# Weight buffers at four different places modulo 512 bytes, in a two-layer decoder trunk

## The chip, the cores and the metric

The kernel runs on one core of one Trainium2 chip. The metric is the device time of one execution, in microseconds. Two runs of the kernel before took 1301.53 and 1301.77 us, median 1301.65 us. TensorE appears as PE (matmuls) and PEld (loads of the stationary operand), VectorE as DVE, ScalarE as ACT, GpSimd as POOL, SyncE as SP; SPq and ACTq are the DMA-issuing instructions of these engines.

## The reference, cut to what matters

Two layers over 256 positions of width 2048, all in float32. The even layer projects x with one wide matrix, feeds a state-space mixer (SSD) and a causal attention over one block of 256 positions, joins both and projects back. The odd layer is a diagonal complex state-space mixer (S5) with a gated unit (GLU) between two projections. Each ends in a LayerNorm.

```python
def reference(x, ...):
    for layer in range(DEPTH):                      # DEPTH = 2
        if layer % 2 == 0:
            h = ssd_moba_mixer(x, in0_w, ..., out0_w)   # x @ w_in ... concat([y_a, y_b]) @ w_out
        else:
            h = s5_mixer(x, in1_w, ..., glu_w, out1_w)  # x @ w_in, scan, gelu(y) @ w_glu, ... @ w_out
        x = layer_norm(DEEPNORM_ALPHA * x + h, ln_g[layer], ln_b[layer])
    return x
```

## The kernel before, in words

**Units of weights.** All projections read their weights in units of 128 partitions x 1024 float32 (4096 bytes per partition). `split_to` (L252) issues, for each unit, one DMA from SP into a buffer `raw` (L275), then `split` (L242) makes two parts of it in TensorE's fp32r format: ACT copies the unit to `wh` (the high part, L236) and DVE subtracts, `wl = raw - wh` (the low part, L244). The three tags `raw`, `wh` and `wl` lie in the pool `st` (L184) with four buffers each. A few units, whose numbers lie in `keep[1]`, get buffers of their own in another pool, because they are used twice or late.

**Products.** A product of float32 accuracy is the sum of three fp32r matmuls: high by high, high by low, low by high. In `xmm` (L323) the activations are the stationary operand (128 columns, 512 bytes per partition) and the weights stream through, 512 columns (2048 bytes) a matmul. In `pairmm` (L331, L334) the weights are stationary, and the activations stream through: 512 columns for the high part of the weights, 256 for the low part. The GLU's groups 1 to 3 have a form of their own (L1624, with weights streaming). The activations lie in the large slots `AB`, `CF` and `D`.

**What sets the order.** The program is written as a sequence of calls; a scheduler then fixes the order of instructions on each engine, from the calls' order, a simulated timeline and the moment at which a buffer of a pool comes free there. On the chip each engine runs its list strictly in that order and waits on semaphores. Before the change a new `wh` or `wl` takes whichever of the four buffers of its tag comes free first; so the order of the buffers is not a fixed rotation, and where two units are used out of turn the later one needn't wait for the earlier.

**Addresses.** In the program as built, the four `raw`, the four `wh` and the four `wl` all start at multiples of 512 bytes in a partition (`wh` at 119808, 123904, 128000 and 132096), and so do `AB`, `CF` and `D`. The slices that the fp32r matmuls read are 512 bytes, 1024 bytes or 2048 bytes long and start at such multiples too. A tile `pad` of 160 bytes in the first pool (L479) sets where the rest begins.

**Two places that the text below speaks of.** (1) The output projection of the even layer, 641 to 727 us into the span, where POOL, DVE and SP also prepare tables for the odd layer: `bc`, a tile of 256 KB, is loaded by SP at L806; DVE reads it at L820 and L821 into `tm`, and sums `tm` into `bb` at L823; `ft` and `bb` go through small matmuls at L857. (2) The change from one GLU group to the next, some 1158 us into the span: `end` (L1652 to L1657) adds the PSUM tiles of the group on DVE, and the next group's first matmul writes the PSUM bank that L1654 has read.

Of the kernel before, what the change touches and what calls it, by code (L numbers as in the profile page):

```python
# [9 lines left out]
F32 = mybir.dt.float32  # L10
F32R = mybir.dt.float32r
# [5 lines left out]
P = 128  # L17
# [3 lines left out]
UK = 2  # L21
# [4 lines left out]
STEPS = [0, 1, 4, 2, 5, 6, 3, 7]  # L26
WARM0 = 10
PAD = 40
FIRST = 3
EPS = 1e-5  # L30
NEG = -1e30
# [139 lines left out]
def trunk(tc, io, out):  # L171
# [4 lines left out]
    def nm(s):  # L176
        count[0] += 1
        return f"{s}_{count[0]}"

    with ExitStack() as top:  # L180
# [3 lines left out]
        st = enter(tc.tile_pool(name="st", bufs=4))  # L184
# [19 lines left out]
        def big(tag, shape, dt=F32):  # L204
            return slot.tile(shape, dt, tag=tag, name=nm(tag))

        units = []
        for name in ("wi0", "wo0", "wi1", "wglu", "wo1"):
            units += [io[name][i] for i in range(io[name].shape[0])]
# [5 lines left out]
        keep = [None, range(0)]  # L215
# [35 lines left out]
        def split_to(i):  # L251
            while nsplit[0] <= min(i, len(units) - 1):  # L252
                n = nsplit[0]
                if n in early:
                    early.pop(n)()
                if n in special:
                    special.pop(n)(n)
                    continue
                raw = st.tile([P, UK, 512], F32, tag="raw", name=nm("raw"))
                if n == 0:  # L260
                    wh = st.tile([P, UK, 512], F32R, tag="wh", name=nm("wh"))
                    wl = st.tile([P, UK, 512], F32R, tag="wl", name=nm("wl"))
                    for k in range(UK):
                        chained(nc.sync, nc.sync.dma_start, raw[:, k, :], units[n][:, k * 512 : k * 512 + 512])
                    for k in range(UK):
                        xpart(k)
                        chained(A, A.activation, wh[:, k, :], raw[:, k, :], AF.Copy)
                        chained(V, V.tensor_tensor, wl[:, k, :], raw[:, k, :], wh[:, k, :].bitcast(F32), op=OP.subtract)
                    ready[n] = (wh, wl)
                    nsplit[0] += 1  # L270
                    continue
                if n == FIRST + 1:
                    for e in (nc.sync, A, V):
                        line.pop(e, None)
                f = chained if nc.sync in line else lambda e, f, *a: f(*a)  # L275
                lastraw[0] = f(nc.sync, nc.sync.dma_start, raw.rearrange("p k n -> p (k n)"), units[n])
                at = room.get(n, n)
                pool, th, tl = (keep[0], f"wh{at % 8}", f"wl{at % 8}") if at in keep[1] else (st, "wh", "wl")
                wh = pool.tile([P, UK, 512], F32R, tag=th, name=nm("wh"))
                wl = pool.tile([P, UK, 512], F32R, tag=tl, name=nm("wl"))  # L280
                split(n, raw, wh, wl)

        jobs = deque()
# [200 lines left out]
        with ExitStack() as l0:  # L484
# [172 lines left out]
            ta = fmem[:, 2304:3072].rearrange("p (a n) -> p a n", a=3)  # L657
            tb = fmem[:, 3072:4096].rearrange("p (a n) -> p a n", a=4)
# [504 lines left out]
        with ExitStack() as lt:  # L1163
            tp = lt.enter_context(tc.tile_pool(name="tp", bufs=1))
# [128 lines left out]
        with ExitStack() as l1:  # L1293
# [287 lines left out]
            forms, fx, gp, set0 = more["f"], more["x"], more["p"], more["s"]  # L1581

            def fast_unit(raws, second):
                def go(n):
                    raw = st.tile([P, UK, 512], F32, tag="raw", name=nm("raw"))
                    lastraw[0] = nc.sync.dma_start(raw.rearrange("p k n -> p (k n)"), units[n])
                    if not second:
                        wh, wl = (st.tile([P, UK, 512], F32R, tag=t, name=nm(t)) for t in ("wh", "wl"))
                        raws[0] = raw
                        split(n, raw, wh, wl)  # L1590
                        return
                    wh, wl = (fx.tile([P, 1, 512], F32R, tag=t, bufs=2, name=nm(t)) for t in ("bh", "bl"))
                    ra = raws[0]
                    ta, tb = (fx.tile([P, 2, 512], F32, tag="mix", bufs=2, name=nm("mix")) for _ in range(2))
                    V.tensor_tensor(ta, ra, raw[:, 1:2, :].to_broadcast([P, 2, 512]), op=OP.subtract)
                    V.tensor_tensor(tb[:, 0, :], ta[:, 1, :], ra[:, 0, :], op=OP.add)
                    V.tensor_tensor(tb[:, 1, :], raw[:, 0, :], tb[:, 0, :], op=OP.subtract)
                    got = [(wh, wl)]
                    A.activation(wh[:, 0, :], raw[:, 0, :], AF.Copy)
                    V.tensor_tensor(wl[:, 0, :], raw[:, 0, :], wh[:, 0, :].bitcast(F32), op=OP.subtract)  # L1600
                    for t, pool, bufs in ((ta, fx, 2), (tb, st, 4)):
                        th, tl = (pool.tile([P, UK, 512], F32R, tag=tag, bufs=bufs, name=nm(tag)) for tag in ("wh", "wl"))
                        high = A.activation(th, t, AF.Copy)
                        low = V.tensor_tensor(tl, t, th.bitcast(F32), op=OP.subtract)
                        got.append((th, tl))
                    splits[n] = (high, low)
                    ready[n] = got
                    nsplit[0] += 1
                return go
# [122 lines left out]
        with ExitStack() as l2:  # L1732
# [56 lines left out]
            def last():  # L1789
                t = 1  # L1790
                mr = mr1[:, t]
                chain = []

                def then(f, *args, **kw):
                    with ExitStack() as pin:
                        if chain:
                            pin.enter_context(tc.issue_after(chain[-1].ins))
                        chain.append(f(*args, **kw))

                pf = [tpp.tile([P, 512], F32, name=f"tail{i}")[:, 0:NB] for i in range(2)]  # L1800
                for i in range(2):
                    T.matmul(pf[i], ident, xg[:, i, :], start=True, stop=False)
                low, high = x1[:, t, 1536 : 1536 + S], x1[:, t, 1536 + S :]
                then(V.scalar_tensor_tensor, x1[:, t, 1536:], x1[:, t, 1536:], ALPHA, ps_t[t][t], op0=OP.mult, op1=OP.add)
                then(V.bn_stats, st1[:, t, 3, :], low)
                then(V.tensor_tensor, high, high, ps_t[t][2][:, S:], op=OP.add)
                then(V.bn_stats, st1[:, t, 4, :], high)
                then(V.bn_aggr, mr[:, 0:2], st1[:, t, :, :].rearrange("p a b -> p (a b)"))
                then(V.tensor_scalar, mr[:, 2:3], mr[:, 1:2], EPS, None, op0=OP.add)
                dg = tp.tile([P, 2, P], F32, name="dg")  # L1810
                first = A.activation(dg[:, 0, :], ident, AF.Copy, scale=mr[:, 0:1])
                with tc.issue_after(first.ins):
                    root = A.activation(mr[:, 3:4], mr[:, 2:3], AF.Sqrt)
                with tc.issue_after(root.ins):
                    A.activation(dg[:, 1, :], ident, AF.Copy, scale=mr[:, 3:4])
                sls = [slice(2 * NB + sum(NV[:i]), 2 * NB + sum(NV[: i + 1])) for i in range(len(NV))]

                def centre(i):
                    xv = x1[:, t, sls[i]]
                    then(V.scalar_tensor_tensor, xv, xv, mr[:, 0:1], gb1[:, 0, sls[i]], op0=OP.subtract, op1=OP.mult)  # L1820

                def rescale(i):
                    xv = x1[:, t, sls[i]]
                    then(V.scalar_tensor_tensor, xv, xv, mr[:, 2:3], gb1[:, 1, sls[i]], op0=OP.mult, op1=OP.add)
                    nc.sync.dma_start(out[t * P : t * P + P, sls[i]], xv)

                centre(0)
                then(V.reciprocal, mr[:, 2:3], mr[:, 3:4])
                for i in range(2):
                    T.matmul(pf[i], dg[:, 0, :], gn[:, i, :], start=False, stop=False)  # L1830
                for i in range(2):
                    T.matmul(pf[i], dg[:, 1, :], gb1[:, 1, NB * i : NB * i + NB], start=False, stop=True)
                rescale(0)
                for i in range(1, len(NV)):
                    centre(i)
                    rescale(i)
                for i in range(2):
                    sl = slice(NB * i, NB * i + NB)
                    A.activation(x1[:, t, sl], pf[i], AF.Copy, scale=mr[:, 2:3])
                    nc.scalar.dma_start(out[t * P : t * P + P, sl], x1[:, t, sl])  # L1840
# [29 lines left out]
```

## Time and profile before

| what | value |
|---|---|
| median of the two runs | 1301.65 us |
| the profiled execution's own time | 1301.36 us |
| its span (first to last instruction) | 1299.5 us |
| around the span (the difference) | 1.9 us |
| matmuls, busy PE | 7998, 1292.1 us |
| busy DVE, ACT, POOL | 1038.5, 704.6, 424.5 us |
| granted TensorE clock, mean | 0.999 |
| splits on ACT (L236), mean of one | 425, 1058 ns |
| splits on DVE (L244), mean of one | 425, 1251 ns |

A matmul's duration in the profile (about 390 ns for 512 columns) contains its latency; what a matmul costs when it stands in a row of others is the distance from its start to the next one's start. The chain of work that ended last counts it so: in a row of it, the time divided by the count is the cost of one.

### The profile page before, as it was taken

The numbers are of one execution on the slowest core, as the hardware profiler recorded it, in microseconds if no ns is written. First come the engines' busy times: TensorE is split into PE (matmuls) and PEld (weight loads), VectorE is DVE, ScalarE is ACT, GpSimd is POOL, SyncE is SP. The second block draws the span as 40 slices with busy tenths as digits, with TensorE's granted clock in tenths as the row PEclk, the third lists the DMA queues.
The fourth block names the chain that finished last, engine by engine and source line by source line (L and its number), as shares of the span: only waits on it lengthen the run. The fifth ranks groups of instructions, "written<-read, shape, count | busy, mean of one in ns | idle before, by whom it ended". The sixth has DMA issues, their size and how long they took to land.

```text
span 1299.5 us, 21574 instructions
## 1 busy us (share of the span) xinstructions
PE 1292.1 (99%) x7998; PEld 1093.2 (84%) x7998; DVE 1038.5 (80%) x1575; ACT 704.6 (54%) x972; POOL 424.5 (33%) x665
## 2 busy tenths in 40 slices
PE   9999999999999999999999999999999999999998
PEld 8888888887888888888888888888888888888886
DVE  6889848798798788889878766749998857878876
ACT  6666669965654544544554345743355555554442
POOL 0060000124028659749788720034432200000100
PEclk9999999999999999999999999999999999999999
DMA  8655675555657857858867787497988665556872
GB/s 324 199 163 179 198 264 194 159 182 179 208 186 248 261 190 251 271 178 269 304 219 250 241 264 248 138 345 241 328 307 297 209 222 184 183 185 227 279 227 94
DMA packets 92106, 295.47 MB, mean 227 GB/s; under 512 B 11536, under 2 KB 18704, under 8 KB 91744
## 3 DMA queue, kind: packets, MB, share of 16 engines
q1 hardware_dynamic: 73696, 249.57, 58.1%
q0 software_dynamic: 8224, 32.81, 7.4%
q10 hardware_dynamic: 10080, 11.71, 2.9%
q8 instruction: 63, 1.03, 0.3%
q14 instruction: 43, 0.35, 0.1%
HBM read 272.78 MB, written 21.27 MB: 226 GB/s over the span
## 4 chain that ended last, share of the span: by engine, by line
PE 96%; POOL 2%; DVE 1%; ACT 1%; issue 0%; DMA 0%; ACTq 0%; POOLq 0%
PE main L323 37%; PE main L331 26%; PE main L334 13%; PE more L1624 7%; PE main L1624 3%; PE main L1263 2%; PE aux L331 1%; PE aux L956 1%; POOL CF L573 1%; PE aux L857 1%; POOL CF L572 1%; PE enc L1383 1%; PE dec L1428 1%; PE aux L334 1%; PE aux L459 1%; PE aux L1043 1%
## 5 line engine op out<-in xcount | busy, mean ns | idle before, releaser
L236 ACT ACTIVATE wh<-raw 128x1024 fp32r<-128x1024 f32 x425 | 447.8, 1058 | 447.7 <-PE main L323 176.4
L244 DVE TENSOR_TENSOR wl<-raw,wh 128x1024 fp32r<-128x1024 f32 x425 | 529.5, 1251 | 195.2 <-ACT wh L236 189.4
L331 PE MATMUL main<-AB,wh 128*128 128x512 f32 x1344 | 347.2, 394 | 0.0
L331 PEld LDWEIGHTS main<-AB,wh 128*128 128x128 f32 x1344 | 238.7, 189 | 41.6 <-issue 1.1
L323 PE MATMUL main<-wh,CF 128*128 128x512 f32 (+1 forms) x768 | 240.0, 391 | 0.0
L334 PEld LDWEIGHTS main<-AB,wl 128*128 128x128 f32 x1344 | 189.5, 190 | 17.4 <-issue 0.2
L323 PE MATMUL main<-wh,AB 128*128 128x512 f32 x640 | 202.0, 392 | 0.0
L334 PE MATMUL main<-AB,wl 128*128 128x256 f32 x1344 | 196.7, 283 | 0.0
L323 PEld LDWEIGHTS main<-wh,CF 128*128 128x128 f32 x768 | 143.7, 188 | 30.0
L323 PE MATMUL main<-wl,CF 128*128 128x512 f32 x384 | 149.4, 389 | 0.0
L323 PEld LDWEIGHTS main<-wh,AB 128*128 128x128 f32 x640 | 120.1, 188 | 25.9 <-issue 0.6
L786 POOL TENSOR_TENSOR c<-c 128x8 f32<-128x8 f32 (+2 forms) x192 | 126.0, 675 | 36.8 <-DMA wb<-c 29.3
L323 PE MATMUL main<-wl,AB 128*128 128x512 f32 x320 | 124.6, 390 | 0.0
L323 PEld LDWEIGHTS main<-wl,CF 128*128 128x128 f32 x384 | 72.1, 188 | 14.6
L1624 PE MATMUL more<-wh,AB 128*128 128x512 f32 x228 | 76.7, 391 | 0.0
L323 PEld LDWEIGHTS main<-wl,AB 128*128 128x128 f32 x320 | 60.1, 188 | 12.0
L1023 POOL TENSOR_TENSOR a<-a,b 64x512 f32<-64x512 f32 x16 | 29.5, 1845 | 119.3 <-DVE a L1022 99.9
L788 POOL TENSOR_TENSOR c<-c,c 128x4 f32<-128x4 f32 (+2 forms) x96 | 59.3, 617 | 7.4
L789 POOL TENSOR_TENSOR c<-c,c 128x4 f32<-128x4 f32 (+2 forms) x96 | 60.1, 626 | 0.0
L965 POOL TENSOR_TENSOR ssq<-ssq,c 128x256 f32<-128x256 f32 x16 | 21.3, 1329 | 109.9 <-ACT c L963 109.3
L331 PE MATMUL main<-CF,wh 128*128 128x512 f32 x192 | 50.4, 397 | 0.0
L1624 PEld LDWEIGHTS more<-wh,AB 128*128 128x128 f32 x228 | 42.7, 188 | 8.9
(354 smaller groups left out, 1617.4 us busy)
## 6 DMA issues: line engine op xcount, KB each, us to landing
raw<-in_wi SPq DMA_DIRECT2D x271, 512.0 KB, 4.3
raw<-in_wo SPq DMA_DIRECT2D x96, 512.0 KB, 4.5
raw<-in_wglu SPq DMA_DIRECT2D x64, 512.0 KB, 3.8
wt<-wb POOLq DMA_DIRECT2D x16, 896.0 KB, 7.7
a<-cumd SPq DMA_DIRECT2D x8, 512.0 KB, 7.1
bc<-in_s5bc SPq DMA_DIRECT2D x16, 256.0 KB, 5.2
bt<-in_s5bt SPq DMA_DIRECT2D x16, 256.0 KB, 5.6
lt<-qd SPq DMA_DIRECT2D x32, 128.0 KB, 5.3
```

Source lines behind the costliest of these rows:

```text
L236: ins = A.activation(wh, raw, AF.Copy)
L244: low = V.tensor_tensor(wl, raw, wh.bitcast(F32), op=OP.subtract)
L323: end = T.matmul((ps[o] if acc is None else acc)[:, cs], l[:, k, sl], r[:, j, cs], start=start and i == 0, stop=stop and i == 2, skip_grou ...
L331: T.matmul(ps[o].rearrange("p (a n) -> p a n", a=2), wh[:, j, sl], x2[:, :, k, :], start=start, stop=False, skip_group_check=True)
L334: T.matmul(ps[o][:, 0:S], wl[:, j, sl], x2[:, 0, k, :], start=False, stop=stop, skip_group_check=True)
L786: G.tensor_tensor(p[:, :, :, 0:m], cs[:, :, :, 1 : m + 1], cs[:, i, :, n : n + 1].unsqueeze(1).to_broadcast([P, 2, 4, m]), op=OP.mult)
L788: G.tensor_tensor(cs[:, 0, :, n + 1 : n + 1 + m], p0[:, 0, :, 0:m], p1[:, 1, :, 0:m], op=OP.subtract)
L789: G.tensor_tensor(cs[:, 1, :, n + 1 : n + 1 + m], p0[:, 1, :, 0:m], p1[:, 0, :, 0:m], op=OP.add)
L965: G.tensor_tensor(ssq, ssq, jk[:, f, :], op=OP.add)
L1023: turns.append(G.tensor_tensor(q[0:64], q[0:64], tm, op=OP.add))
L1263: end = T.matmul(ps[t], l[:, k, sl], r[:, j, :], start=k == 0 and i == 0, stop=k == KT - 1 and i == 2)
L1624: lastmm[0] = T.matmul(ps[name], l, r, start=start and i == 0, stop=last and i == 2, skip_group_check=True)
```

## The change

Each tag `wh` and `wl` is replaced by four tags with one buffer each, handed out in fixed turns by a counter (`weights`). Behind the low part's buffers lie 64, 192, 128 and 0 bytes that nothing uses. In the program as built the four pairs (high and low part alike) then start 0, 64, 256 and 384 bytes behind multiples of 512: `wh` at 119808, 128064, 136448 and 144768. The 384 bytes in all push every pool behind `st` by 384, so the kept units, and all the working tiles of the layers, start 384 bytes further modulo 512 than before. `raw`, `AB`, `CF` and `D` stay. Since this takes 384 bytes more, the small tile `dg` of the last LayerNorm moves into a `raw` buffer.

```diff
+GAPS = [16, 48, 32, 0]
...
+        given = {"wh": 0, "wl": 0}
+
+        def weights(tag):
+            i = given[tag] % 4
+            given[tag] += 1
+            t = st.tile([P, UK * 512 + (GAPS[i] if tag == "wl" else 0)], F32R, tag=f"{tag}{i}", bufs=1, name=nm(tag))
+            return t[:, 0 : UK * 512].rearrange("p (k n) -> p k n", n=512)
+
...
-                    wh = st.tile([P, UK, 512], F32R, tag="wh", name=nm("wh"))
-                    wl = st.tile([P, UK, 512], F32R, tag="wl", name=nm("wl"))
+                    wh, wl = weights("wh"), weights("wl")
...
-                pool, th, tl = (keep[0], f"wh{at % 8}", f"wl{at % 8}") if at in keep[1] else (st, "wh", "wl")
-                wh = pool.tile([P, UK, 512], F32R, tag=th, name=nm("wh"))
-                wl = pool.tile([P, UK, 512], F32R, tag=tl, name=nm("wl"))
+                if at in keep[1]:
+                    wh, wl = (keep[0].tile([P, UK, 512], F32R, tag=f"{t}{at % 8}", name=nm(t)) for t in ("wh", "wl"))
+                else:
+                    wh, wl = weights("wh"), weights("wl")
...
-                        wh, wl = (st.tile([P, UK, 512], F32R, tag=t, name=nm(t)) for t in ("wh", "wl"))
+                        wh, wl = weights("wh"), weights("wl")
...
-                    for t, pool, bufs in ((ta, fx, 2), (tb, st, 4)):
-                        th, tl = (pool.tile([P, UK, 512], F32R, tag=tag, bufs=bufs, name=nm(tag)) for tag in ("wh", "wl"))
+                    for t, pool in ((ta, fx), (tb, st)):
+                        th, tl = (weights(tag) if pool is st else fx.tile([P, UK, 512], F32R, tag=tag, bufs=2, name=nm(tag)) for tag in ("wh", "wl"))
...
-                dg = tp.tile([P, 2, P], F32, name="dg")
+                dg = st.tile([P, UK, 512], F32, tag="raw", name=nm("raw"))[:, :, 0:P]
```

The fixed turns also move instructions. SP's list stays as it is, and most of the other lists; the differences lie at the two places named above and in the GLU groups around them. In the rows below, the number at the end of a name is the running number of its buffer, and a unit is called by that of its `wh` (`wl_7277` is the low part of unit 7276); behind the change a line's number is 9 higher (8 for SP's).

At the first place, PE's list before the change, from the end of unit 7246 on: unit 7276 begins, then unit 7174 (the last of the product before, `main_6739` and `main_6740`) comes in between, then 7276 goes on.

```order
L323 MATMUL main_7273<-wl_7247,CF_3604 128x512
L323 MATMUL main_7273<-wh_7246,CF_3604 128x512
L323 MATMUL main_7272<-wh_7276,CF_3604 128x512
L323 MATMUL main_7272<-wl_7277,CF_3604 128x512
L323 MATMUL main_7272<-wh_7276,CF_3604 128x512
L323 MATMUL main_6739<-wh_7174,CF_3604 128x512
L323 MATMUL main_6739<-wl_7175,CF_3604 128x512
```

The same after the change, from the last matmuls of unit 7174 on:

```order
L332 MATMUL main_6740<-wl_7175,CF_3604 128x512
L332 MATMUL main_6740<-wh_7174,CF_3604 128x512
L866 MATMUL aux_7519<-ft_7238,bb_7215 64x64 x8
L332 MATMUL main_7272<-wh_7276,CF_3604 128x512
L332 MATMUL main_7273<-wh_7276,CF_3604 128x512
L332 MATMUL main_7272<-wl_7277,CF_3604 128x512
```

Unit 7174 now runs whole (12 matmuls) ahead of 7276, and eight small matmuls of L866 (L857 before), which stood some 80 rows later, stand between them. Units 7174 and 7276 have the same buffer in the fixed turn.

DVE's list at the same place before the change:

```order
L843 TENSOR_TENSOR et_7262<-et_7262,te_7263 128x4x64
L244 TENSOR_TENSOR wl_7277<-raw_7274,wh_7276 128x1024
L1084 TENSOR_TENSOR a_1026_6489<-aux_6952,a_1026_6489 128x512
L831 COPY ft_7238<-bc_7208 128x128
L832 TENSOR_TENSOR ft_7238<-bc_7208,lam 128x128x3
```

And after it, some fifteen rows further down:

```order
L843 TENSOR_TENSOR ft_7238<-ft_7238,tm_7239 128x128x3
L253 TENSOR_TENSOR wl_7369<-raw_7366,wh_7368 128x1024
L829 TENSOR_TENSOR tm_7392<-bc_7384,wri 128x128
L830 TENSOR_TENSOR tm_7392<-bc_7384,wri 128x128
L832 TENSOR_TENSOR bb_7391<-tm_7392 128x512
L253 TENSOR_TENSOR wl_7277<-raw_7274,wh_7276 128x1024
L1150 SCALAR_TENSOR_TENSOR D_7271<-a_1169_7292,main_6739 128x512
```

The low part of unit 7276 was made ahead of those of 7300, 7318 and 7368; now these three come first, and so do three instructions that read the freshly loaded tile `bc_7384`. The places of 7276, 7300 and 7318 in DVE's list of before are taken over by 7300, 7318 and 7368. ACT's list moves in the same way: the high part of 7276 now stands behind that of 7368 and behind four DMA issues of ACT (`wb<-om` and `wb<-ft`).

At the second place, DVE's list before the change, around the sums that end GLU group 2:

```order
L244 TENSOR_TENSOR wl_12019<-raw_12016,wh_12018 128x1024
L1649 TENSOR_TENSOR gt_12013<-p_1971_12010,more_11865 128x512
L1654 TENSOR_TENSOR gt_12008<-more_11719,gt_12008 128x512
L1652 TENSOR_TENSOR gt_12013<-main_11715,gt_12013 128x512
L1656 TENSOR_TENSOR p_1969_12007<-more_11723,p_1969_12007 128x512
L1657 TENSOR_TENSOR p_1971_12010<-more_11727,p_1971_12010 128x512
L244 TENSOR_TENSOR wl_12049<-raw_12046,wh_12048 128x1024
```

And after it:

```order
L253 TENSOR_TENSOR wl_12019<-raw_12016,wh_12018 128x1024
L1657 TENSOR_TENSOR p_1971_12010<-p_1971_12010,main_11869 128x512
L253 TENSOR_TENSOR wl_12049<-raw_12046,wh_12048 128x1024
L1658 TENSOR_TENSOR gt_12013<-p_1971_12010,more_11865 128x512
L1663 TENSOR_TENSOR gt_12008<-more_11719,gt_12008 128x512
```

The split of unit 12048, which stood behind all the sums, now stands ahead of the sum of `more_11719` (L1654 before, L1663 after). PE's list goes through the 12 matmuls of unit 11976 and then to `more_12068<-wh_12003`, whose bank is that of `more_11719`, in both programs; unit 12048 has the buffer of unit 11958, the one ahead of 11976.

## The prediction

> **What bounds the kernel now.** I read the page's busy times first, then the chain of work that ended last, then what PE waited for.
>
> ```profile
> span 1299.5 us, 21574 instructions
> PE 1292.1 (99%) x7998; PEld 1093.2 (84%) x7998; DVE 1038.5 (80%) x1575; ACT 704.6 (54%) x972; POOL 424.5 (33%) x665
> PEclk9999999999999999999999999999999999999999
> PE 96%; POOL 2%; DVE 1%; ACT 1%; issue 0%; DMA 0%; ACTq 0%; POOLq 0%
> PE main L323 37%; PE main L331 26%; PE main L334 13%; PE more L1624 7%; PE main L1624 3%; PE main L1263 2%; PE aux L331 1%; PE aux L956 1%; POOL CF L573 1%; PE aux L857 1%; POOL CF L572 1%; PE enc L1383 1%; PE dec L1428 1%; PE aux L334 1%; PE aux L459 1%; PE aux L1043 1%
> ```
>
> PE sets the time from end to end: 96% of the chain, at full clock. Matmuls through which weights stream (L323, L1624, L1263) hold 37+7+3+2 = 49% of the span, 637 us; those with stationary weights hold 26% (L331, 338 us) and 13% (L334, 169 us). So a change counts in two ways only: it alters what one matmul costs in a row of others, or it makes PE wait. PE hardly waits now (whom PE waited for, its first rows):
>
> ```profile
> PE aux L468 <- POOL D L463: 1.3, 1, 1.3
> PE tail L1830 <- ACT dg L1811: 0.5, 1, 0.5
> ```
>
> What a matmul costs, from pieces of the chain and, in the last two rows, the timeline:
>
> ```profile
> 1163.17 2.04 PE more L1624 x9
> 198.98 1.84 PE main L331 x8
> 200.82 0.95 PE main L334 x8
> 686.22 0.43 PE aux L1076 x2
> 687.52 1.08 PE aux L857 x32
> ```
> ```profile
> 682.88 0.62 PE L323 MATMUL main<-wh,CF 128*128 128x512 f32 x2
> 682.88 0.19 PEld L323 LDWEIGHTS main<-wh,CF 128*128 128x128 f32 x1
> ```
>
> 512 streamed columns cost 227 ns, in L331's form 230 ns, 256 columns 119 ns. An fp32 matmul of 256 columns is done in two passes, each as long as 512 fp32r columns, and a pass costs 215 ns. So an fp32r matmul pays about 11 ns that an fp32 pass doesn't, and the load of the next stationary operand starts with it, in the same hundredth of a microsecond.
>
> **The change, part by part.** (1) *The turns at the output projection.* Unit 7276 may be split only when unit 7174 has left their common buffer, and its low part stands on DVE behind the instructions that read `bc_7384`. Timeline of before, with the landing time of that tile's transfer, in three views:
>
> ```profile
> 693.65 0.61 PE L323 MATMUL main<-wh,CF 128*128 128x512 f32 x2
> 694.13 1.06 ACT L236 ACTIVATE wh<-raw 128x1024 fp32r<-128x1024 f32 x1 [1.66 <-PE main L323]
> 694.53 0.96 SPq L806 DMA_DIRECT2D bc<-in_s5bc  x1
> 694.95 0.81 ACTq L877 DMA_DIRECT2D wb<-om  x2
> 695.86 1.29 ACTq L848 DMA_DIRECT2D wb<-ft  x2
> ```
> ```profile
> DMA to landing us min/median/max: 5.4/5.4/5.4
> ```
> ```profile
> 690.77 0.29 DVE L820 TENSOR_TENSOR tm<-bc,wri 128x128 f32<-128x128 f32 x1
> 690.98 0.29 DVE L821 TENSOR_TENSOR tm<-bc,wri 128x128 f32<-128x128 f32 x1
> 691.20 0.61 DVE L871 SCALAR_TENSOR_TENSOR om<-aux,consts,om 128x384 f32<-128x384 f32 x1
> 691.72 0.68 DVE L823 TENSOR_TENSOR bb<-tm 128x512 f32<-128x512 f32 x1
> 692.32 0.47 DVE L871 SCALAR_TENSOR_TENSOR om<-aux,consts,om 128x256 f32<-128x256 f32 x1
> 695.25 1.27 DVE L244 TENSOR_TENSOR wl<-raw,wh 128x1024 fp32r<-128x1024 f32 x1
> 700.46 0.54 DVE L820 TENSOR_TENSOR tm<-bc,wri 128x128 f32<-128x128 f32 x1
> 700.92 0.54 DVE L821 TENSOR_TENSOR tm<-bc,wri 128x128 f32<-128x128 f32 x1
> 701.39 1.21 DVE L244 TENSOR_TENSOR wl<-raw,wh 128x1024 fp32r<-128x1024 f32 x1
> ```
>
> PE leaves unit 7246 with the first matmul of the row 693.65, so at 693.65 + 0.23 = 693.88. Then come 12 matmuls of 7174 (12 x 0.227 = 2.72, to 696.60), 16 passes of small matmuls (half of the chain's 1.08 us for 32, 0.54, to 697.14), and two matmuls on the high part of 7276 (0.45). The first on its low part would start at 697.6. ACT can't help in time either: its four DMA issues end at 695.86 + 1.29 = 697.15, then 1.06 us of copy, 698.2. But the low part is later: SP's list is the same and its waits here are for splits that keep their times (7300, 7318 and 7368 take over the places of 7276, 7300 and 7318), so `bc_7384` is issued at 694.53 and lands at 699.9. DVE, done with 7368 at 696.5, stands before it. Then come L820 and L821 (0.21+0.22 from start to start in the quiet case, 0.46+0.47 in the slower one of 700.46), L823 (0.60 to the next row) and the split (1.21): 702.2 to 702.7. PE loses **4.6 to 5.1 us; I take 4.9**. Its cover is gone since nothing else stands ahead of unit 7276 on PE. What is queued behind the waiting DVE instruction: the residual sums of `main_6739` and `main_6740` (L1141) and the split of 7398, which PE needs only three units, 8 us, later. So the delay doesn't breed another.
>
> (2) *The turns at the end of GLU group 2.*
>
> ```profile
> 1148.75 1.06 ACT L236 ACTIVATE wh<-raw 128x1024 fp32r<-128x1024 f32 x1 [1.65 <-PE more L1624]
> 1149.84 1.22 DVE L244 TENSOR_TENSOR wl<-raw,wh 128x1024 fp32r<-128x1024 f32 x1 [0.52 <-ACT wh L236]
> 1154.83 1.22 DVE L244 TENSOR_TENSOR wl<-raw,wh 128x1024 fp32r<-128x1024 f32 x1
> 1155.97 0.68 DVE L1649 TENSOR_TENSOR gt<-p,more 128x512 f32<-128x512 f32 x1
> 1156.57 0.68 DVE L1654 TENSOR_TENSOR gt<-more,gt 128x512 f32<-128x512 f32 x1
> ```
>
> The sum that frees the bank of the next group's first matmul now stands behind the split of unit 12048, whose buffer unit 11958 leaves 12 matmuls (2.72 us) ahead of that matmul. From then: ACT 1.09 to DVE's start, 1.14 to L1649, 0.60 to L1654, 0.68 to its end: 3.5 us. PE waits for the rest, **0.8 us** (0 if ACT had begun earlier, 1.1 with the semaphores).
>
> (3) *The places of the buffers, on PE.* No fp32r matmul of 512 columns in the trace of before reads at anything but a multiple of 512 bytes, so the trace has no row for this; it is the large unknown, since three quarters of the units move. The nearest rows are of fp32: L1076, whose streamed tile `b` starts 32 bytes behind a multiple of 512, costs 0.43 us for its two passes (above), and L647, with both operands at multiples of 512, the same 0.43 (89.66 to 90.09):
>
> ```profile
> 89.66 0.60 PE L647 MATMUL aux<-a,a 128*128 128x256 f32 x2
> 90.09 0.38 PE L648 MATMUL aux<-a,a 128*128 128x128 f32 x2
> ```
>
> So I take **0**. The bounds: the best is that every moved matmul loses its surplus over an fp32 pass: 3/4 x 637 x (227-215)/227 = 25 us, L331 3/4 x 338 x (230-215)/230 = 17, L334 3/4 x 169 x (119-107.5)/119 = 12, together 54 us. The worst that the rows suggest is the same surplus a second time, +54 us.
>
> (4) *What is hidden.* The splits write to other places too (the costliest group of DVE, whom DVE waits for most, whom SP's queue waits for most):
>
> ```profile
> L244 DVE TENSOR_TENSOR wl<-raw,wh 128x1024 fp32r<-128x1024 f32 x425 | 529.5, 1251 | 195.2 <-ACT wh L236 189.4
> DVE wl L244 <- ACT wh L236: 189.4, 180, 5.1
> SPq L275 <- DVE wl L244: 758.3, 321, 10.7
> ```
>
> DVE is idle for 20% of the span, most of it in waits for the next high part, so a few per cent on its splits stay behind PE's work; without that cover 5% would be 0.05 x 529.5 = 26 us. SP's transfers wait for buffers and not the other way round, so their new places cost nothing. `dg` moves to a `raw` buffer whose last split is long done: the 0.5 us of L1830 stay.
>
> **The sum:** 1301.4 (profiled execution, 0.3 under the median of the runs) + 4.9 + 0.8 + 0; from the median 1301.65 it is **1307.3 us**.
>
> **Rivals.** *The clock falls in the gap.* At the start the clock shows what a restart costs:
>
> ```profile
> 1.32 3.96 PE L468 MATMUL aux<-D 128*128 128x512 f32 x10 [1.32 <-POOL D L463]
> ```
>
> Ten matmuls take 3.96 us there instead of 2.27, 1.7 us more. If the wait of 4 us within part (1) puts PE back into that state, the time is 1309.0. Against it: in before no wait of PE after the start exceeds 0.5 us, so nothing shows that a wait of 4 us is enough. [...]
>
> *The moved places make matmuls cheaper.* Load and stream start together, and today both always start at the same place modulo 512; if that is what costs the 11 ns, moving them apart returns some. For it speaks the unexplained surplus, and that L331 costs 3 ns more than L1624 for the same columns; against it that the fp32 rows show no effect. At half of the bound, 27 us: 1280. It puts the time below the median of before as soon as it is worth more than 5.7 us, 0.7% of the 858 us (3/4 of 637+338+169) that move. [...]
>
> *They make matmuls dearer*, in the same way: a stream of 2048 bytes that starts off a multiple of 512 touches one more such block, and loads of 512 bytes touch two. At half of the bound: 1334. It is over 2% slower from 20 us on, 2.4% of those 858 us.
>
> *No wait arises at the first place*, because the high part of 7276 runs early enough and DVE gets `bc_7384` in time; it would take a transfer of about 1 us in place of 5.4. Then the time is 1302.4.
>
> **How the numbers follow.** Order alone, places neutral: 0.48, 1307.3. Clock falls: 0.10, 1309. Cheaper matmuls: 0.17, 1280. Dearer: 0.20, 1334. No wait: 0.05, 1302.4. For the two cases of places I let small effects be likelier than large, falling in a straight line to nothing at 54 us. Below 1292 then lies 0.17 x (38.7/54)² = 0.09, above 1324 0.20 x (37.3/54)² = 0.10; so the range is 1292 to 1324. The likeliest case has 1305 to 1309 for itself. A measurement of this kernel tells about 2% from no change: 26 us, so below 1275.6 or above 1327.7. The same triangle gives 0.17 x (22.3/54)² = 0.03 faster and 0.20 x (33.6/54)² = 0.08 slower, and 0.89 within.
>
> **What would show it.** In the profile after, part (1) is right if PE waits some 4 us for DVE `wl` in one piece around 699 us, between an L332 matmul on a high part and the next on a low part, and DVE ahead of it for the transfer of `bc`. Part (2) is right if PE waits about 0.8 us for DVE some 1160 us into the span. Part (3) is right if a piece of the chain still gives 227 ns for L1633 (L1624 before), 230 for L340 and 119 for L343. Any other distance there, multiplied by the counts, is the part that I got wrong; a granted clock below 1 behind the gap would be the first rival.

## The result, and the profile after

The changed kernel takes 1317.67 us (median of two runs, 1317.65 and 1317.69), 16.0 us more than the 1301.65 us of the kernel before: a ratio of 1.0123, 95% interval 1.0080 to 1.0167. Forecast were 1307.3 us, and a range of 1292 to 1324. Lines L323, L331, L334, L1624 of before are L332, L340, L343, L1633 now.

The page of after: span, PE's busy time and the chain's shares by engine.

```profile
span 1315.9 us, 21576 instructions
PE 1303.4 (99%) x7998; PEld 1092.2 (83%) x7998; DVE 1036.3 (79%) x1575; ACT 704.5 (54%) x972; POOL 421.9 (32%) x665
PE 94%; DVE 2%; POOL 2%; ACT 1%; issue 1%; DMA 1%; DVEq 0%; ACTq 0%; POOLq 0%
```

The same 7998 matmuls keep PE busy for 11.3 us longer (1292.1 before), and the chain's shares of DVE and DMA have grown from 1% and 0% to 2% and 1%. So there are two effects: dearer matmuls, and waits. Whom PE waits for (us in total, times, longest):

```profile
PE main L332 <- DVE wl L253: 3.0, 1, 3.0
PE aux L477 <- POOL D L472: 1.3, 1, 1.3
PE more L1633 <- DVE gt L1663: 0.9, 1, 0.9
PE main L332 <- ACT wh L245: 0.9, 1, 0.9
PE tail L1839 <- ACT raw L1820: 0.6, 1, 0.6
```

Three of these rows are new: 3.0 and 0.9 us at the output projection, and 0.9 us at the end of GLU group 2. The chain at the first place (start, us, what):

```profile
695.46 4.26 DMA bc<-in_s5bc
...
699.82 0.70 DVE tm L829
700.51 0.21 DVE tm L830
...
701.50 1.48 DVE wl L253
702.97 0.04 issue
703.02 9.00 PE main L332 x31
```

It is the order that the prediction read: the transfer, the two products, the sum (L832, 700.75 to 701.50), the split, and PE. What happened to the clock stands in a table by stretches (span, then for each engine busy time and count, the granted clock, the DMA share and GB/s):

```profile
690.00:697.00 7.00, 7.00 (x32) 5.70 (x31) 7.00 (x15) 3.45 (x4) 6.53 (x14) 1.00 0.69 207
697.00:703.70 6.70, 2.81 (x25) 1.73 (x24) 4.30 (x7) 1.06 (x1) 5.75 (x15) 1.00 0.75 248
703.70:707.10 3.40, 3.40 (x10) 2.59 (x9) 1.65 (x3) 0.17 (x1) 2.10 (x11) 0.54 0.59 187
```

Less than 1 us after PE goes on (at 703.02) the granted clock falls to one half (0.50 from 703.96 to 707.37) for 3.4 us; the row says 0.54 because it begins a little ahead of that. It holds ten matmuls, with room for fifteen at 227 ns; the steps within it are 426 or 427 ns. At the GLU's end the chain is the predicted one too:

```profile
1169.01 1.07 ACT wh L245
1170.08 0.02 issue
1170.10 1.23 DVE wl L253
1171.33 0.60 DVE gt L1658
1171.92 0.61 DVE gt L1663
1172.53 0.14 issue
1172.67 2.56 PE more L1633 x10
```

What a matmul costs shows in long pieces of the chain. First a piece of before, then the one of after that starts at nearly the same time, and two of after for the stationary weights:

```profile
729.80 14.96 PE main L323 x66
```
```profile
729.89 22.82 PE main L332 x99
190.50 1.84 PE main L340 x8
192.34 0.95 PE main L343 x8
```

14.96/66 = 227 ns has become 22.82/99 = 230.5 ns where the weights stream. The two pieces with stationary weights look as before. To see more I took from the traces the distance from each matmul's start to the next one's, where one follows the other without a pause, with the places of both operands, and call it the step. Mean step before and after: streamed weights, 512 columns, 227.1 and 230.7 ns; stationary weights, high part 230.7 and 231.5, low part 118.7 and 117.3. With the counts (2661, 1561, 1555) that is +9.6, +1.3 and -2.2 us: **8.7 us of dearer matmuls**, spread over the whole span.

### The profile page after: what moved, and what is told of

Read it like the earlier page. It is cut to its first block, busy times and chain, and to the rows that moved or that the text cites. A ratio compares the mean times of both kernels' runs of the same rounds, so it can differ in the third digit from the quotient of the medians.

```text
span 1315.9 us, 21576 instructions
## 1 busy us (share of the span) xinstructions
PE 1303.4 (99%) x7998; PEld 1092.2 (83%) x7998; DVE 1036.3 (79%) x1575; ACT 704.5 (54%) x972; POOL 421.9 (32%) x665
## 4 chain that ended last, share of the span: by engine, by line
PE 94%; DVE 2%; POOL 2%; ACT 1%; issue 1%; DMA 1%; DVEq 0%; ACTq 0%; POOLq 0%
PE main L332 36%; PE main L340 26%; PE main L343 13%; PE more L1633 7%; PE main L1633 3%; PE main L1272 2%; PE aux L340 1%; PE aux L965 1%; POOL CF L582 1%; POOL CF L581 1%; PE enc L1392 1%; PE dec L1437 1%; PE aux L343 1%; PE aux L866 1%; PE aux L468 1%
## 5 line engine op out<-in xcount | busy, mean ns | idle before, releaser
L340 PE MATMUL main<-AB,wh 128*128 128x512 f32 x1344 | 348.2, 395 | 0.0
L340 PEld LDWEIGHTS main<-AB,wh 128*128 128x128 f32 x1344 | 238.1, 188 | 41.9 <-issue 1.2
L332 PE MATMUL main<-wh,CF 128*128 128x512 f32 (+1 forms) x768 | 244.5, 396 | 0.9 <-ACT wh L245 0.9
L332 PE MATMUL main<-wh,AB 128*128 128x512 f32 x640 | 204.4, 395 | 0.0
L343 PEld LDWEIGHTS main<-AB,wl 128*128 128x128 f32 x1344 | 188.0, 189 | 18.2 <-issue 0.2
L343 PE MATMUL main<-AB,wl 128*128 128x256 f32 x1344 | 194.7, 281 | 0.0
L332 PEld LDWEIGHTS main<-wh,CF 128*128 128x128 f32 x768 | 144.4, 189 | 33.5 <-ACT wh L245 1.0
L332 PE MATMUL main<-wl,CF 128*128 128x512 f32 x384 | 150.9, 393 | 3.0 <-DVE wl L253 3.0
L332 PEld LDWEIGHTS main<-wh,AB 128*128 128x128 f32 x640 | 120.1, 188 | 27.8 <-issue 0.6
L795 POOL TENSOR_TENSOR c<-c 128x8 f32<-128x8 f32 (+2 forms) x192 | 123.3, 660 | 34.0 <-DMA wb<-c 26.5
L332 PE MATMUL main<-wl,AB 128*128 128x512 f32 x320 | 125.2, 391 | 0.0
L332 PEld LDWEIGHTS main<-wl,CF 128*128 128x128 f32 x384 | 72.6, 189 | 19.6 <-DVE wl L253 3.4
L1633 PE MATMUL more<-wh,AB 128*128 128x512 f32 x228 | 77.9, 394 | 0.9 <-DVE gt L1663 0.9
L332 PEld LDWEIGHTS main<-wl,AB 128*128 128x128 f32 x320 | 60.1, 188 | 13.1
L1633 PEld LDWEIGHTS more<-wh,AB 128*128 128x128 f32 x228 | 42.7, 188 | 11.0 <-issue 1.3
L340 PE MATMUL main<-CF,wh 128*128 128x512 f32 x192 | 50.5, 397 | 0.0
```

What stands on the lines that cost most here:

```text
L332: end = T.matmul((ps[o] if acc is None else acc)[:, cs], l[:, k, sl], r[:, j, cs], start=start and i == 0, stop=stop and i == 2, skip_grou ...
L340: T.matmul(ps[o].rearrange("p (a n) -> p a n", a=2), wh[:, j, sl], x2[:, :, k, :], start=start, stop=False, skip_group_check=True)
L343: T.matmul(ps[o][:, 0:S], wl[:, j, sl], x2[:, 0, k, :], start=False, stop=stop, skip_group_check=True)
L795: G.tensor_tensor(p[:, :, :, 0:m], cs[:, :, :, 1 : m + 1], cs[:, i, :, n : n + 1].unsqueeze(1).to_broadcast([P, 2, 4, m]), op=OP.mult)
L1633: lastmm[0] = T.matmul(ps[name], l, r, start=start and i == 0, stop=last and i == 2, skip_group_check=True)
```

## The experiments

Ratios are to the kernel before, run beside each on the same chip (1301.7 to 1301.9 us). All kernels compute the whole reference.

**Order and places apart.** `turns_alone` has the fixed turns without the gaps:

```diff
-GAPS = [16, 48, 32, 0]
+GAPS = [0, 0, 0, 0]
```

> The fixed turns with no gaps: all weight buffers at multiples of 512, instructions in the order of the changed kernel. Theory A (order and places both cost): the waits of PE for the low part of unit 7276 (about 3.9 us), at the end of GLU group 2 (0.9 us) and a granted clock of one half for about 3.4 us behind the first (1.7 to 3 us) stay, every streamed matmul is back at 227 ns, and the time is 1301.65 + 7 to 8 = 1309 to 1310 us. Rival B (the order alone, the longer distances between matmuls are a consequence of the waits): 1317 us, with 230 to 232 ns still there. Rival C (places alone): 1302 us.

Measured: 1308.64 us, ratio 1.0057 (1.0044 to 1.0070), +6.9 us. Streamed steps are back at 227.2 ns, the waits stay:

```profile
PE main L332 <- DVE wl L253: 1.9, 1, 1.9
PE main L332 <- ACT wh L245: 1.5, 1, 1.5
...
PE more L1633 <- DVE gt L1663: 1.0, 1, 1.0
```
```profile
702.50:705.90 3.40, 3.40 (x11) 2.61 (x10) 1.44 (x3) 0.63 (x1) 2.08 (x11) 0.55 0.48 161
```

The second fence is again the row of a stretch of 3.4 us, with half the clock (0.55). Set against the trace of before, matmul by matmul, this run is 0.07 us late until the first place, gains 5.8 us of delay there, 1.3 us at the end of the GLU group, and nothing anywhere else. The 5.8 are 3.4 of waits and about 1.7 of the clock; the waits are counted from the modelled end of a matmul, 0.16 us behind the point where the next one would have started (0.39 us long, at a step of 0.23), which for two waits gives 0.3 more. The first matmul behind each wait takes 341 ns in place of 227, which gives 0.2 more; some 0.2 us are left over.

`places_alone` has the gaps, but takes the buffers in the turn in which the kernel before took them (a table of the calls at which its rotation skips):

```diff
-GAPS = [16, 48, 32, 0]
+GAPS, SKIP = [16, 48, 32, 0], {227: 1, 369: 1, 370: 2, 371: 1, 373: 1, 374: 2, 375: 1, 377: 1, 378: 2, 379: 1, 381: 1, 382: 2, 383: 1}
...
-            i = given[tag] % 4
+            i = (given[tag] + sum(v for k, v in SKIP.items() if k <= given[tag])) % 4
```

> The gaps stay, the turns follow the order in which the kernel before took its buffers, so the instructions stand as before (but for some twenty matmuls of one GLU group). Theory A: no wait of PE over 0.6 us, full clock throughout, 230 to 232 ns for streamed matmuls at offsets 64, 256 and 384, and the time is 1301.65 + 8 = 1309 to 1311 us. Rival B: 1302 us with 227 ns. Rival C (places alone make the whole difference): 1317 us.

Measured: 1310.89 us, ratio 1.0071 (1.0057 to 1.0084), +9.2 us. PE's longest new wait is one of 0.7 us among the first units; the dear matmuls are all there, 17.27/75 = 230.3 ns:

```profile
PE aux L477 <- POOL D L472: 1.3, 1, 1.3
PE aux L340 <- ACT wh L245: 0.7, 1, 0.7
PE tail L1839 <- ACT raw L1820: 0.6, 1, 0.6
```
```profile
729.84 17.27 PE main L332 x75
```

6.9 + 9.2 = 16.1, and the whole change cost 16.0: order and places add up, and theory A holds against B and C, but for its limit of 0.6 us on PE's waits.

**What makes the wait and the clock.** `bc_late` is `turns_alone` with the three DVE instructions on `bc` moved a step back, behind the split of unit 7276:

```diff
                     with tc.issue_after(lastraw[0].ins):
                         loads()
-                    wides()
+                    pass
...
                 def fcs():
-                    bc = h["bc"]
+                    wides(); bc = h["bc"]
```

> As turns_alone (fixed turns, no gaps), but the three DVE instructions that read the fresh tile for bb stand with those of ft, one step later in the program, so that the split of unit 7276 no longer stands behind them. Theory D (DVE's wait for that transfer makes the long wait of PE, and the two waits together make the clock fall): of the 1308.6 us of turns_alone the 1.9 us of waiting for the low part go, and the 1.7 us of the halved clock with them, the 1.5 us of waiting for the high part on ACT stay: 1305.0 us. Rival E (the low part is late for another reason, ACT's own lateness): 1308.6 us. If the shorter wait still makes the clock fall: 1306.7 us.

Measured: 1305.5 us, ratio 1.0029 (1.0017 to 1.0040). The long wait for `wl` is gone; a wait of the same length now stands 16 small matmuls ahead of it, for the tile `ft`, while the wait for ACT is gone:

```profile
PE aux L866 <- DVE ft L843: 1.9, 1, 1.9
PE aux L477 <- POOL D L472: 1.3, 1, 1.3
```
```profile
700.90:704.30 3.40, 3.40 (x10) 2.62 (x9) 2.01 (x4) 0.00 (x0) 0.10 (x1) 0.51 0.99 337
```

So theory D's cause is right (the split is late because of the readers of `bc` ahead of it), though not its bookkeeping of which wait stays. The seven executions also price the clock: the profiled one, 1307.38 us, shows the half clock behind the wait (0.51 above); the six others took 1305.13 to 1305.94, median about 1305.5. That they kept the full clock is an inference from their times, 1.9 us less, where half speed for 3.4 us costs 1.7.

**Which places cost.** The remaining runs keep the order of before and, but for `low_64` and `stat_64`, give all weights one distance from the activations. Most of their edits are one tile ahead of the weight buffers (`all_64`, on the changed kernel with the table of `places_alone` and no gaps):

```diff
                 if n == 0:
-                    wh, wl = weights("wh"), weights("wl")
+                    st.tile([P, 16], F32, tag="shift", bufs=1, name="shift"); wh, wl = weights("wh"), weights("wl")
```

> Order of before, no gaps, but a tile of 64 bytes ahead of the weight buffers: every weight buffer and the kept units lie 64 bytes behind a multiple of 512, the activations at multiples of 512. Theory A1 (the offset of a streamed operand itself costs, whatever its neighbours have): about 3.3 ns for each of some 2780 streamed matmuls of 512 columns, 9 us, less about 1 us at the stationary weights, so 1309 to 1311 us. Rival A2 (what costs is that the offset changes from unit to unit): 227 ns again and 1301.7 us, within 1 us.

`whole_64` moves the activations along instead:

```diff
-PAD = 40
-GAPS = [16, 48, 32, 0]
+PAD = 56
+GAPS, SKIP = [0, 0, 0, 0], {227: 1, 369: 1, 370: 2, 371: 1, 373: 1, 374: 2, 375: 1, 377: 1, 378: 2, 379: 1, 381: 1, 382: 2, 383: 1}
```

> Order of before, no gaps, and the pad in the first pool is 64 bytes longer, so that the activation slots, the raw buffers and the weight buffers all lie 64 bytes behind multiples of 512. Theory A3 (what counts is each operand's own place modulo 512): as with the weights alone at 64 or dearer, since the streamed activations of the stationary-weight products are moved too: 1310 to 1320 us. Rival A4 (what counts is the distance of the streamed operand from the stationary one, modulo 512): 227, 230 and 119 ns as before and 1301.7 us, within 1 us.

Measured: `all_64` 1303.36 us, ratio 1.0014 (1.0005 to 1.0023); `whole_64` 1301.73 us, 1.0000 (0.9991 to 1.0009). A place of 64 costs nothing if both operands have it: A4 holds, and A3 falls. And a distance of 64 everywhere costs 1.7 us, not the 9 of A1, since the low matmuls gain more than expected and the streamed ones lose less (table below); A2's 1301.7 within 1 us is missed too. Pieces of the chain of `all_64` and `whole_64`, 228.9 and 226.6 ns:

```profile
729.98 13.05 PE main L332 x57
```
```profile
729.80 15.41 PE main L332 x68
```

`all_256` (on the kernel before; `all_384` has 96 in place of 64, on the form of `all_64`):

```diff
                 if n == 0:
-                    wh = st.tile([P, UK, 512], F32R, tag="wh", name=nm("wh"))
+                    st.tile([P, 64], F32, tag="shift", bufs=1, name="shift"); wh = st.tile([P, UK, 512], F32R, tag="wh", name=nm("wh"))
```

> The kernel before with a tile of 256 bytes ahead of the high buffers: all weights 256 bytes behind a multiple of 512, the activations at multiples of 512. Theory A1 (each distance has its own price, read from the mixed run behind its first matmuls: some 229.3 ns for a streamed matmul, half a nanosecond less for the stationary ones): 2676 x 2.2 = +5.9, less 1.6, 1306 us. Rival A2 (most of the price is that the distance changes from unit to unit): streamed matmuls at 227 to 228 ns and 1301 to 1303 us.

> Order of before, no gaps, a tile of 384 bytes ahead of the weight buffers: all weights 384 bytes behind a multiple of 512, the activations at multiples of 512. Theory A1: streamed matmuls at 233 ns (the mean of the 237 and 229 that alternate in the mixed run), 2676 x 5.9 = +15.8 us, about nothing at the stationary ones: 1317 us. Rival A2: 227 to 229 ns and 1301 to 1306 us.

Measured: `all_256` 1301.89 us, 1.0001 (0.9992 to 1.0010): a distance of 256 is no distance. `all_384` 1318.73 us, 1.0130 (1.0116 to 1.0144): A1's 1317, dear for every streamed matmul, 21.84/94 = 232.3 ns:

```profile
729.78 15.41 PE main L323 x68
```
```profile
729.97 21.84 PE main L332 x94
```

`low_64` moves the low parts alone (the tile stands behind the four `wh`):

```diff
-                    wh = st.tile([P, UK, 512], F32R, tag="wh", name=nm("wh"))
+                    wh = st.tile([P, UK, 512], F32R, tag="wh", name=nm("wh")); st.tile([P, 16], F32, tag="shift", bufs=1, name="shift")
```

> The kernel before with a tile of 64 bytes between the high and the low buffers: high parts at multiples of 512, low parts 64 bytes behind (the kept units, both parts, too). Theory A5 (the cost of a matmul depends on the distance modulo 512 between the stream that runs and the operand that is loaded beside it): with stationary weights a low part that is loaded beside an unshifted stream makes the 256-column matmuls 4.25 ns cheaper, in 7 of 8 cases, 1360 x 4.25 = 5.8 us, and nothing is lost at the high parts but 0.4 us at the changes; the streamed low parts, a third of 2676, cost 1.9 ns each, 1.7 us. Together 1301.7 - 3.7 = 1298.0 us. Rival A6 (what the low matmuls gain is only what the high ones lose, booked elsewhere): 1301.7 + 1.7 = 1303.4 us.

Measured: 1312.34 us, 1.0081 (1.0068 to 1.0095): both expectations missed by 9 us and more. In this run two of three streamed matmuls have the distance 0 and one 64, and both kinds take 231.9 ns, more than in a run that has only the one (227.1) or only the other (229.1):

```profile
729.95 16.95 PE main L323 x73
```

The second of two high parts in a row, with no change of distance ahead of it, takes 231.6 ns too. So **a change of the distance costs by itself**, and not only at the matmul where it happens. After shows the same: the first four matmuls of a unit at offset 0 that follows one at 384 have steps of 232, 232, 231 and 227 ns (medians in the trace), then 227; a unit at 256, as free as 0 when alone, settles only at its eleventh matmul.

`all_192` and `all_32` (48 and 8 in place of 64 in the edit of `all_256`) try other distances:

> The kernel before with a tile of 192 bytes ahead of the high buffers: all weights 192 behind a multiple of 512, activations at multiples. If what counts is the distance modulo 256 (256 gave the same as 0), this is a distance of -64. Mirrored costs: streamed matmuls at 229 ns, low ones at 114.5, 1303.4 us. Costs that grow with the distance between the operands rather than modulo 256: above the 1318.7 us of all_384 or between 1303 and 1318.

> The same with 32 bytes. If the price rises in steps of 64 bytes: 1301.7 us (as 0) or 1303.4 us (as 64). If it follows the distance in a line: half of all_64's +1.7 us, 1302.6 us; streamed matmuls at 228 ns, low ones at 116.6 ns.

Measured: `all_192` 1313.16 us, 1.0088 (1.0074 to 1.0101), not the mirror image of `all_64`; `all_32` 1320.62 us, 1.0144 (1.0130 to 1.0158), the dearest of all, neither a step of 64 nor a line. To know whether the signed distance counts or the places, `acts_64` reaches the distance of `all_192` with both operands elsewhere (`PAD` 56, and the tile of `all_256` with 48):

> The kernel before with 64 bytes more ahead of the activation slots and 192 bytes more ahead of the weights: activations 64 behind multiples of 512, weights 256 behind multiples of 512, which is the distance of all_192 (weights less activations, modulo 256) with other places for both. If only the signed distance modulo 256 counts: as all_192, 1313.2 us, streamed matmuls at 233.2 ns, high ones at 229.8, low ones at 116.5. If the distance counts without its sign: as all_64, 1303.4 us, 229.1, 232.6 and 114.5 ns. If the place of the weights alone counts: as all_256, 1301.9 us.

Measured: 1313.34 us, 1.0090 (1.0076 to 1.0104), the same as `all_192` in every step. Chain pieces of `all_192`, `all_32` and `acts_64`, 233.3, 233.4 and 233.3 ns:

```profile
729.91 15.63 PE main L323 x67
```
```profile
729.86 22.41 PE main L323 x96
```
```profile
729.95 15.63 PE main L323 x67
```

Mean steps (ns) by the place of the weights less that of the activations, modulo 256; the times are differences of medians. That modulo 256 is the right measure rests on one pair, 0 and 256; a distance of 128 itself was not run:

| distance | run | weights stream, 512 | high stationary, 512 | low stationary, 256 | time |
|---|---|---|---|---|---|
| 0 | before | 227.1 | 230.7 | 118.7 | |
| 0 | whole_64, all_256 | 227.1 | 230.7 | 118.8 | 0.0, +0.1 us |
| 32 | all_32 | 233.2 | 232.5 | 118.8 | +18.7 us |
| 64 | all_64 | 229.1 | 232.6 | 114.5 | +1.7 us |
| 384 (128 modulo 256) | all_384 | 232.4 | 232.5 | 118.6 | +16.9 us |
| 192 | all_192, acts_64 | 233.2 | 229.8 | 116.5 | +11.3, +11.7 us |

**A version that beats both.** The table's best entry for stationary weights, of the two that leave the streamed weights cheap, is 64. `stat_64` gives it to most of them and 0 to most streamed ones: the slot `AB` gets 64 bytes of slack, so that everything behind it moves by 64, and its contents start 64 bytes later only where weights stream past them:

```diff
-        def big(tag, shape, dt=F32):
-            return slot.tile(shape, dt, tag=tag, name=nm(tag))
-
+        def big(tag, shape, dt=F32, at=0):
+            t = slot.tile([P, int(np.prod(shape[1:])) + GAP] if tag == "AB" else shape, dt, tag=tag, name=nm(tag))
+            return t if tag != "AB" else t[:, at : at + int(np.prod(shape[1:]))].rearrange("p (a k s) -> p a k s" if len(shape) == 4 else "p (a s) -> p a s", a=2, **({"k": KT} if len(shape) == 4 else {}))
...
-            ya = big("AB", [P, 2, KT, S], F32R)
+            ya = big("AB", [P, 2, KT, S], F32R, at=GAP)
```

(`yy` likewise; `GAP` is 16.)

> Order of before; the slot AB is 64 bytes longer, so that CF, the raw buffers, all weights and the kept units lie 64 bytes behind multiples of 512; AB itself is used at a multiple of 512 where its contents stream past stationary weights, and 64 bytes behind where the weights stream past it. So the products with stationary weights on AB (1408 of 1600 pairs of matmuls) have the distance 64, and all the others the distance 0. Theory A7 (each stretch of products pays for its own distance alone): high ones 230.7 to 232.6 ns, low ones 118.75 to 114.5 ns as in all_64, streamed ones 227.1 ns as before: 1301.75 - 1408 x 2.33 ns = 1298.5 us. Rival A8 (the gain of the low matmuls in all_64 is a matter of that run's mixture with what follows): 1301.7 us or more.

Measured: 1299.31 us, ratio 0.9979 (0.9970 to 0.9988), 2.6 us less than before. The costliest groups on PE with stationary weights, of before and of this run (busy time, mean of one, idle before):

```profile
L331 PE MATMUL main<-AB,wh 128*128 128x512 f32 x1344 | 347.2, 394 | 0.0
L334 PE MATMUL main<-AB,wl 128*128 128x256 f32 x1344 | 196.7, 283 | 0.0
```
```profile
L331 PE MATMUL main<-AB,wh 128*128 128x512 f32 x1344 | 349.7, 396 | 0.0
L334 PE MATMUL main<-AB,wl 128*128 128x256 f32 x1344 | 191.0, 278 | 0.0
```
```profile
729.95 12.69 PE main L323 x56
```

+2.5 and -5.7 us: 3.2 us won, as A7 said. The rest of the gap to its 1298.5 lies in 369 streamed matmuls whose next operand to load still lies at 0: their step is 229.1 ns, 0.7 us in all. In this run `raw` lies with the weights, so what these matmuls pay for is the distance to the activations and not that to `raw`. Nor do the other engines make the price: in `all_384`, 104 streamed matmuls run while DVE, ACT and POOL do nothing, and their step is 232.4 ns as well. Elsewhere in `stat_64` streamed weights are back at 12.69/56 = 226.6 ns.

## Why the prediction was right and where it was wrong

- **What bounds the kernel: right.** Nothing moved the time but PE's steps, PE's waits and PE's clock.
- **Part (1), the turns at the output projection: right in mechanism, 4.9 us forecast.** The transfer, L829 to L832, and the split end the wait as worked out. The waits were 3.0 + 0.9 = 3.9 us, and not one piece: 0.9 us were for the high part on ACT, which the sum left out because the low part would be later. `bc` was issued 0.9 us later than forecast but landed after 4.26 us in place of 5.4; and PE itself came later, because by then the dear matmuls had delayed it by 0.9 us.
- **Part (2), the end of GLU group 2: right in mechanism, a little small.** 0.8 us forecast (1.1 at most), a wait of 0.9, and 1.2 to 1.3 us of delay from start to start.
- **The clock rival: it came true**, with 0.10 given to it. The price of 1.7 us, taken from the start of the span, was right (1.7 by the half clock, 1.9 between the executions of `bc_late`), in part by luck: at the start 0.4 us of it was the long first step (594 ns in place of 227), and only the five behind it took 427 ns, as those at the half clock of after do. The argument against it, that no wait of before exceeded 0.5 us, was only a lack of rows. The half clock of after lasted 3.4 us (0.50); the stretches of 3.4 us in `turns_alone` and `bc_late` have means of 0.55 and 0.51. In `bc_late` the clock fell behind one wait of 1.9 us, and the longest single one of `turns_alone` is 1.9 us too, so one wait of 4 us isn't needed; how short a wait is enough no run shows.
- **Part (3), the places: the step that failed is "So I take 0".** It measured 9.2 us alone, nearly all of it dearer matmuls. The rows under it were of fp32 matmuls, of which the one with a streamed tile 32 bytes off cost no more (0.43 us for two passes, as without the 32 bytes); with fp32r operands 32 bytes are the dearest distance tried, 6 ns a streamed matmul (233.2 against 227.1). A row of another form of instruction priced the term, and the 0 came from that row alone. The rival "they make matmuls dearer" was the true one, at 9 us in place of the 27 that half the bound gave. That a place can move the 11 ns or so between an fp32 pass (215) and an fp32r matmul (227), from which the bound was made, was the author's assumption. The rival's picture (a stream that starts off a multiple of 512 touches one more block) falls, since `whole_64` has every operand off such a multiple and costs nothing (1301.73 us). The rival "cheaper" was right in kind for one group: low stationary parts gain 4 ns at a distance of 64 (114.5 against 118.7 ns). The steps of streamed matmuls differ by the distance alone, 227 to 233 ns; where in the chip the difference arises no run shows.
- **How after's share comes about.** With the steps of the table for each unit's own distance, the streamed matmuls of after would lose 601 x 2.0 + 836 x 5.3 ns = 5.6 us; they lose 9.6. The other 4.0 us are put down to the changes from one distance to the next, which the fixed turns make at every unit; no run takes them apart from the rest.
- **The sum.** 5.7 us of order were forecast, and the order cost 6.9 with the clock; 0 of places, and they cost 9.2: 1.2 and 9.2 make up the 10.4 us between 1307.3 and 1317.67. The range held because it was drawn from the bounds of part (3), wide enough for an effect that the sum put at nothing; that the time fell within it is luck and not a confirmation of the sum. The likeliest case's own range, 1305 to 1309, did not hold, and two rivals came true together, the clock and dearer matmuls, which no case of the prediction had joined.

What stays open is why the distance counts. The runs show that it counts with its sign (streamed steps of 229.1 ns at 64 and 233.2 at 192, which is -64 modulo 256), that 256 bytes are as good as 0 (1301.89 us against 1301.82), and that a change of it costs (231.9 ns in `low_64`, where 0 and 64 are mixed); not by which circuit.

## What to carry to other kernels

When the fp32r matmuls of a product follow each other without a pause, keep the streamed and the loaded operands at one distance modulo 256 bytes, and keep it the same from buffer to buffer (that 256 counts as 0 rests on one run, 1301.89 us): 0 was the cheapest for streamed weights here (227.1 ns), and mixing 0 with 64 was dearer than either (231.9 ns against 227.1 and 229.1). A buffer's turn is part of the schedule: read which late unit would get the buffer of which late reader, and what stands ahead of its refill on DVE. Price an unknown by a row of the same form of instruction, or leave it unpriced and let the bounds speak.

## What the runs showed of the hardware that was not expected

- The step of a streamed fp32r matmul of 512 columns goes from 227.1 ns (distance 0 or 256 bytes) over 229.1 (64) and 232.4 (384) to 233.2 ns (32 or 192). Moving both operands alike changes nothing (1301.73 us against 1301.7).
- With stationary weights, the distance 64 makes the low part's 256-column matmuls cheaper, 114.5 ns against 118.7, and the high part's dearer, 232.6 against 230.7.
- Half the clock followed waits of PE of 0.9 and 3.0 us (after, 0.50 for 3.4 us), of 1.5 and 1.9 us (`turns_alone`, 0.55 in a stretch of 3.4 us), and a single one of 1.9 us (`bc_late`, in the profiled execution, 0.51 in a stretch of 3.4 us).
